# Scores over full rows, weights as column tiles, and a new split of an expert's weights in a two-block transformer kernel

## The chip, the cores and the metric

The kernel runs on one core of one Trainium2 chip. The metric is the device time of one execution in microseconds, the median of several runs; a profile comes from one further execution, recorded by the hardware profiler. The engines are PE (TensorE, with PEld for its weight loads), DVE (VectorE), ACT (ScalarE), POOL (GpSimd) and SP (SyncE), which issues nearly all DMAs.

## The reference

The input is x (1024 tokens of width 1024), a memory of 256 rows, positions, and the weights of two transformer blocks, all in fp32.

The first block adds to x, in this order: differential attention (8 heads) beside latent attention (8 heads of 64 + 32 dimensions) through one output matrix; cross attention to the memory (4 heads of 128); and a mixture of experts: 32 experts in 4 groups, each token goes to 2 experts of one group, each expert computes `(silu(h @ w_gate) * (h @ w_up)) @ w_down` with inner width 256. A norm closes the block.

The second block projects its normed input with one wide matrix and runs four branches on it:

```python
# fox: 4 heads of 64, causal, with a decay from running sums c of log-sigmoid gates
s = q @ k.T * 64**-0.5 + (c[:, None] - c[None, :]);  p = softmax(where(causal, s, -inf));  o = p @ v
# conv: a short causal convolution with gates, width 256
# mlstm: 4 heads of 64, scores weighted by exponentials of running gate sums, normed, times an output gate
# swa: 8 query heads on 2 key heads, a window of 128 keys, a bucketed position bias, a sink logit per head
```

Each branch has an output matrix; four gates of width 1024 (`tanh` halves in the kernel) weigh their sum, a merge matrix follows, and then a gated feed-forward part of width 2816.

## The kernel before

Precision. The matmuls run in fp32r, and every operand is split in two: a high part (a cast to fp32r, `hi`, on ACT) and a low part (the difference, `lo`, on DVE or POOL). A product is three matmuls, high*high, high*low and low*high (`mm3`, L111 to L113), summed in PSUM.

Weights of the projections. `load_w` (from L93) fetches one column tile of a matrix, 128 columns by `kc` blocks of 128 rows, in chunks of four blocks: one DMA on SP's queue into a `wraw` tile (3 buffers), then `hi` on ACT and `lo` on POOL. In DRAM the matrix lies row by row, so that a chunk is read as runs of 512 bytes, four for each partition.

Order. The Tile framework orders the instructions by a simulated timeline, so that projections (among them the 64 gate units of `gate_halves`, given out in small portions by `gates(n)`) are mixed on PE into the attention of the heads. SP, POOL, ACT, DVE and PE each work through their own queue in order.

Experts. `load(e)` (L1031) issues five DMAs: gate and up in two halves each, and down, into three tiles of `[128, 4, 512]` taken from a ring of twelve. `expert_in` gathers the rows of the expert's tokens with an indirect DMA, transposes and splits them, and multiplies eight weight chunks; `expert_out` applies silu, transposes, and multiplies four more chunks. Each of the twelve chunks goes through `expert_split` (L912): the high part on ACT, or on DVE for chunks 5 and 11, and the low part on POOL for chunks 0, 2, 5, 7 and 10 and on DVE for the others. Both parts lie in rings of four buffers (`whi`, `wlo`).

Scores of the second block. The queries of a head lie as a stack of 128 rows, the high part over the low part (`hq`); the keys as the high part twice (`hk`, 128 rows) and the low part once (`hkl`, 64 rows used). `stack_scores` (L1431) makes the scores of a query block against up to 512 keys with two matmuls: 128 rows (L1433), then the high query rows against the low keys, 64 rows (L1434). Fox adds the decay by a third one, minus ones against the 32 rows of its head in `ck` (L1524), and on the last chunk of a query block the causal mask, an identity of 128 rows (L1526). `attend` runs the query blocks of a head; softmax is on DVE (row maximum) and ACT (exponential), the transposed probabilities are split and multiplied with the values.

Constants. `late_consts` loads among others `iota`, `desc`, `caps` and `tok`, which only the router uses, and makes `nonesr`, the minus ones of fox.

Of the kernel before, what the change touches and what calls it, by code (L numbers as in the profile page):

```python
# [12 lines left out]
F32 = mybir.dt.float32  # L13
F32R = mybir.dt.float32r
# [8 lines left out]
P = 128  # L23
# [39 lines left out]
class K:  # L63
# [29 lines left out]
    def load_w(self, src, kc, f):  # L93

        nc = self.nc
        out = []
        for c0 in range(0, kc, 4):
            n = min(4, kc - c0)
            raw = self.t(self.wp, [P, 4, P], tag="wraw", bufs=3)[:, :n, :f]
            nc.sync.dma_start(raw, src[c0 * P:(c0 + n) * P, :].rearrange("(c p) f -> p c f", p=P))  # L100
            h = self.t(self.wp, [P, 4, P], F32R, tag="whi", bufs=4)[:, :n, :f]
            self.hi(h, raw)
            l = self.t(self.wp, [P, 4, P], F32R, tag="wlo", bufs=4)[:, :n, :f]
            self.lo(l, raw, h, nc.gpsimd)
            out += [(h[:, i], l[:, i]) for i in range(n)]
        return out
# [20 lines left out]
    def late_consts(self):  # L127
# [195 lines left out]
    def out_first(self):  # L323

        nc, tc, a = self.nc, self.tc, self.a
        with tc.tile_pool(name="mxp", bufs=1, side="right") as mp:
            for c in range(8):
                nc.sync.dma_start(self.xs[c], a["xT"][c * P:(c + 1) * P, :])
            for t0 in range(0, S, 512):
# [7 lines left out]
                for c in range(8):  # L337
                    w = self.load_w(a["w_out"][0:512, c * P:(c + 1) * P], 4, P)
# [4 lines left out]
    def out_second(self, mn, t0):  # L343
        nc, a = self.nc, self.a
        for c in range(8):
            w = self.load_w(a["w_out"][512:1024, c * P:(c + 1) * P], 4, P)
# [20 lines left out]
    def latents(self, hh, hl, sp):  # L367

        nc, a = self.nc, self.a
        for f0, f in ((0, P), (P, P), (2 * P, P), (3 * P, 64)):  # L370
            w = self.load_w(a["w_lat"][:, f0:f0 + f], 8, f)
# [7 lines left out]
    def diff_proj(self, j, hh, hl, sp):  # L379

        nc, a = self.nc, self.a
        w = self.load_w(a["w_in"][:, 1024 + j * P:1024 + (j + 1) * P], 8, P)
# [4 lines left out]
        for nmq, off in (("q", 0), ("k", 512)):  # L387
            w = self.load_w(a["w_in"][:, off + j * P:off + (j + 1) * P], 8, P)
# [106 lines left out]
    def mla_proj(self, tp):  # L495
# [58 lines left out]
        def keys(j):  # L554
            pair(self.load_w(a["w_ukv"][:, j * P:(j + 1) * P], 1, P), [ckh], [ckl], self.mkn[j])

        def queries(j):
            pair(self.load_w(a["w_uq"][:, j * P:(j + 1) * P], 2, P), cqh, cql, self.mqn[j])

        def values():  # L560
            wv = self.load_wide(a["w_ukv"][:, 512:1024])
# [20 lines left out]
        for g in range(2):  # L582
            w0 = self.load_w(a["w_uq"][:, 512 + g * P:512 + (g + 1) * P], 2, P)
            w1 = self.load_w(a["w_uq"][:, 768 + g * P:768 + (g + 1) * P], 2, P)
# [48 lines left out]
    def mem_kv(self):  # L633
# [4 lines left out]
        with tc.tile_pool(name="memp", bufs=1, side="right") as mp:  # L638
# [29 lines left out]
    def cross(self):  # L668
# [5 lines left out]
        with ExitStack() as es:  # L674
# [8 lines left out]
            with tc.tile_pool(name="chp", bufs=1, side="right") as hp:  # L683
                for t0 in range(0, S, 512):
# [3 lines left out]
                    for h in range(4):  # L688
                        w = self.load_w(a["w_mem_q"][:, h * P:(h + 1) * P], 8, P)
# [222 lines left out]
    def expert_split(self, pool, ws, n):  # L912
# [103 lines left out]
    def moe(self):  # L1016
# [4 lines left out]
        with self.wes as es:  # L1021
# [228 lines left out]
    OFF = dict(fq=0, fk=256, fv=512, cu=772, cb=1028, cc=1284, mq=1540, mk=1796, mv=2052, mo=2316, sq=2572, sk=3084, sv=3212, gates=3340)  # L1250

    def w2(self, name, j, f=P):
        o = self.OFF[name] + j * P
        return self.load_w(self.a["w_in_2"][:, o:o + f], 8, f)
# [166 lines left out]
    def head_stack(self, pool, d, h, parts, tag):  # L1421

        s = self.t(pool, [P, S], F32R, tag=tag, bufs=2)
# [7 lines left out]
    def stack_scores(self, o, q, ks, k0, kn, last=True):  # L1431
# [15 lines left out]
    def small_cols(self, hh, hl, qp, sp):  # L1447
# [4 lines left out]
        w = self.load_w(a["w_small"], 8, 12)  # L1452
# [55 lines left out]
    def fox(self, sp, j, d, ck):  # L1508
# [213 lines left out]
    def merge(self, yes, yp, sp, first):  # L1722
# [17 lines left out]
        def gated(t0, yh, yl):  # L1740
            hs = slice(t0, t0 + 512)
            mh, ml = ([self.t(mp, [P, 512], F32R, tag=f"{n}{i}") for i in range(8)] for n in ("mh", "ml"))
            for i in range(8):
# [3 lines left out]
                w = self.load_w(a["w_branch"][:, i * P:(i + 1) * P], 10, P)  # L1747
# [10 lines left out]
        def product(t0, mh, ml):  # L1758
            hs = slice(t0, t0 + 512)
            for i in range(8):  # L1760
                x = self.t(mp, [P, 512], tag="xr", bufs=2)
                nc.sync.dma_start(x, self.xd[i * P:(i + 1) * P, hs])
                w = self.load_w(a["w_merge_out_2"][:, i * P:(i + 1) * P], 8, P)
# [33 lines left out]
    def ff_in(self, sp, f0, n, act, fh, halves):  # L1797

        nc, a = self.nc, self.a
        for i in range(n):  # L1800
            cols = slice((f0 + i) * P, (f0 + i + 1) * P)
            w = self.load_w(a["w_gate_2"][:, cols], 8, P)
# [6 lines left out]
            w = self.load_w(a["w_up_2"][:, cols], 8, P)  # L1809
# [22 lines left out]
def layout(inp):  # L1832
# [7 lines left out]
    o["w_in"] = ct(f["w_in"][0])  # L1840
    lat = f["w_in"][0][:, 1536:1952]
    o["w_lat"] = ct(np.concatenate([lat, lat[:, 400:416], lat[:, 384:400]], axis=1))
    uq = f["w_mla_uq"][0].reshape(256, 8, 96)
    o["w_uq"] = ct(np.concatenate([uq[:, :, :64].reshape(256, 512), uq[:, :, 64:].reshape(256, 256),
                                   np.concatenate([uq[:, :, 80:], uq[:, :, 64:80]], axis=2).reshape(256, 256)], axis=1))
    ukv = f["w_mla_ukv"][0].reshape(P, 8, 2, 64)
    o["w_ukv"] = ct(np.concatenate([ukv[:, :, 0].reshape(P, 512), ukv[:, :, 1].reshape(P, 512)], axis=1))
    o["norm_ffn_g"] = ct(f["norm_ffn_g"].reshape(1, D))
    for name in ("w_out", "w_mem_q", "w_mem_kv", "w_mem_o"):
        o[name] = ct(f[name][0])  # L1850
# [33 lines left out]
    for name in ("w_expert_gate", "w_expert_up", "w_expert_down"):  # L1884
        o[name] = f[name][0]
# [8 lines left out]
    o["w_in_2"] = w2  # L1894
    o["w_small"] = ct(np.concatenate([w2[:, 768:772], w2[:, 2308:2312], w2[:, 2312:2316]], axis=1))
    o["b_small"] = ct(np.concatenate([f["fox_f_bias_2"][0], f["mlstm_i_bias_2"][0], f["mlstm_f_bias_2"][0]])[:, None])
    o["w_branch"] = np.concatenate([f[f"w_{n}_out_2"][0] for n in ("fox", "conv", "mlstm", "swa")], axis=0)
    for name in ("w_merge_out_2", "w_gate_2", "w_up_2", "w_down_2"):
        o[name] = f[name][0]
# [28 lines left out]
```

## Time and profile before

| what | value |
|---|---|
| median of 3 runs | 3415.92 us (3400.15 to 3417.51) |
| profiled execution: device time | 3409.51 us |
| profiled execution: span, first to last instruction | 3407.7 us |
| mean granted TensorE clock | 0.956 of 2.4 GHz |
| busy: PE, DVE, ACT, POOL | 3140.9, 1652.7, 1424.3, 1246.6 us |
| moved by DMA | 466.21 MB, mean 137 GB/s |
| packets below 2 KB, of all | 356568 of 442669 |

Busy time of PE counts a pipelined matmul from its start to its modelled end, so that neighbours overlap; the price of a matmul is the time from its start to the start of the next one. The granted clock of a stretch lies between 0.5 (1.2 GHz all the time) and 1.0 (2.4 GHz all the time). Idle time of an engine counts only where that engine sets the pace.

### The profile page before, as it was taken

What the parts mean: (1) busy time and instruction counts of PE and PEld (TensorE: products, weight loads), DVE (VectorE), ACT (ScalarE), POOL (GpSimd) and SP (SyncE); (2) the same over time, 40 slices, a digit from 0 to 9 for tenths busy, and PEclk for the clock granted to TensorE, in tenths of its full rate; (3) what the DMA queues carried; (4) which work ended last, traced back from release to release, by engine and by line L of the source; (5) the groups of instructions that cost most, each with busy time, mean ns of one, the idle gap of its engine ahead of it and who ended that gap; (6) DMA issues with size and microseconds to landing.
All of it is one profiled execution on the core that took longest, in us unless ns stands there. A gap on an engine that the chain in (4) does not pass through costs nothing.

```text
span 3407.7 us, 41840 instructions
## 1 busy us (share of the span) xinstructions
PE 3140.9 (92%) x14621; PEld 2463.5 (72%) x14621; DVE 1652.7 (48%) x3249; ACT 1424.3 (42%) x2839; POOL 1246.6 (37%) x1007
## 2 busy tenths in 40 slices
PE   6998879879968888699999999999999999999999
PEld 4786667767745555577767887778777788888887
DVE  5567985666578888653334454332356311111111
ACT  4555664544536666433333443344344322121121
POOL 3233465555446567531101111111467422222221
PEclk9998889989979999799889999999999999999999
DMA  5654645322369999344343333334565211111112
GB/s 166 212 179 144 245 119 174 91 69 83 111 224 320 329 330 303 133 122 124 96 136 108 106 105 94 92 91 160 158 204 147 85 51 43 52 44 45 51 45 79
DMA packets 442669, 466.21 MB, mean 137 GB/s; under 512 B 28344, under 2 KB 356568, under 8 KB 442456
## 3 DMA queue, kind: packets, MB, share of 16 engines
q1 hardware_dynamic: 436056, 440.44, 41.2%
q0 software_dynamic: 6400, 23.07, 2.2%
q8 instruction: 116, 1.90, 0.2%
q14 instruction: 97, 0.79, 0.1%
HBM read 349.66 MB, written 113.77 MB: 136 GB/s over the span
## 4 chain that ended last, share of the span: by engine, by line
PE 56%; DVE 1%; POOL 1%; DMA 1%; issue 0%; ACT 0%; ACTq 0%; POOLq 0%; DVEq 0%
PE mm L111 16%; PE mm L112 16%; PE mm L113 16%; PE S L1434 2%; PE T L1205 1%; PE S L1433 1%; PE T L1185 1%; PE mm L1089 1%; PE S L1524 1%; PE T L1682 0%; PE mm L164 0%; PE T L1663 0%; DMA wraw<-w_branch 0%; POOL wlo L91 0%; PE T L1104 0%
## 5 line engine op out<-in xcount | busy, mean ns | idle before, releaser
L91 POOL TENSOR_TENSOR wlo<-wraw,whi 128x512 fp32r<-128x512 f32 (+2 forms) x487 | 609.2, 1254 | 1597.6 <-ACT whi L88 1495.2
L111 PE MATMUL mm<-hh,whi 128*128 128x512 f32 (+2 forms) x1968 | 795.0, 404 | 5.5 <-DVE cql L209 2.0
L112 PE MATMUL mm<-hl,whi 128*128 128x512 f32 (+2 forms) x1968 | 793.0, 403 | 6.4 <-POOL hl L91 3.8
L113 PE MATMUL mm<-hh,wlo 128*128 128x512 f32 (+2 forms) x1968 | 790.8, 402 | 0.0
L88 ACT CAST whi<-wraw 128x512 fp32r<-128x512 f32 (+2 forms) x487 | 287.3, 594 | 737.1 <-PE mm L112 629.9
L111 PEld LDWEIGHTS mm<-hh,whi 128*128 128x128 f32 (+2 forms) x1968 | 372.9, 189 | 100.2 <-ACT hh L88 3.4
L112 PEld LDWEIGHTS mm<-hl,whi 128*128 128x128 f32 (+2 forms) x1968 | 372.6, 189 | 99.3 <-POOL hl L91 6.4
L113 PEld LDWEIGHTS mm<-hh,wlo 128*128 128x128 f32 (+2 forms) x1968 | 372.5, 189 | 89.1 <-issue 0.2
L91 POOL TENSOR_TENSOR ptl<-praw,pth 128x512 fp32r<-128x512 f32 (+2 forms) x192 | 205.7, 1075 | 233.4 <-DVE pth L1195 200.7
L91 POOL TENSOR_TENSOR wlo<-w,whi 128x512 fp32r<-128x512 f32 x160 | 225.7, 1416 | 138.8 <-ACT whi L916 106.9
L91 DVE TENSOR_TENSOR wlo<-w,whi 128x512 fp32r<-128x512 f32 x224 | 225.0, 1031 | 22.8 <-ACT whi L916 22.4
L916 ACT CAST whi<-w 128x512 fp32r<-128x512 f32 x320 | 196.2, 622 | 85.5 <-PE mm L113 51.5
L1815 DVE TENSOR_TENSOR ffgate<-ffgate,mm 128x512 f32<-128x512 f32 x44 | 30.2, 687 | 384.7 <-PE mm L113 384.7
L1185 PE MATMUL T<-ident,p 128*128 128x128 f32 x864 | 148.6, 293 | 21.2 <-DVE p L442 8.3
L1826 DVE TENSOR_TENSOR x<-mm,x 128x512 f32<-128x512 f32 x64 | 44.2, 691 | 199.1 <-PE mm L113 199.1
L1185 PEld LDWEIGHTS T<-ident,p 128*128 128x128 f32 x864 | 107.6, 150 | 45.4 <-issue 11.0
L111 PE MATMUL mm<-ah,whi 128*128 128x512 f32 x352 | 139.6, 397 | 0.3 <-DVE x L1826 0.3
L112 PE MATMUL mm<-al,whi 128*128 128x512 f32 x352 | 139.5, 396 | 0.0
L113 PE MATMUL mm<-ah,wlo 128*128 128x512 f32 x352 | 139.5, 396 | 0.0
L91 DVE TENSOR_TENSOR ptl<-T,pth 128x512 fp32r<-128x512 f32 (+2 forms) x128 | 73.1, 578 | 126.0 <-ACT pth L88 96.8
L112 PE MATMUL mm<-wlo,xh 128*112 128x512 f32 x256 | 110.7, 432 | 22.0 <-DVE wlo L91 17.6
L1194 ACT COPY praw<-T 128x512 f32<-128x512 f32 (+2 forms) x192 | 90.5, 478 | 84.2 <-PE T L1185 63.2
(485 smaller groups left out, 5858.4 us busy)
## 6 DMA issues: line engine op xcount, KB each, us to landing
wraw<-w_in SPq DMA_DIRECT2D x152, 256.0 KB, 2.9
w<-w_expert_gate SPq DMA_DIRECT2D x64, 512.0 KB, 6.4
w<-w_expert_up SPq DMA_DIRECT2D x64, 512.0 KB, 7.5
w<-w_expert_down SPq DMA_DIRECT2D x32, 1024.0 KB, 5.6
gd<-gate SPq DMA_DIRECT2D x64, 256.0 KB, 2.0
gt<-gd SPq DMA_DIRECT2D x16, 1024.0 KB, 11.6
yrow<-y SPq DMA_DIRECT2D x32, 448.0 KB, 4.2
wraw<-w_gate SPq DMA_DIRECT2D x48, 256.0 KB
```

Source lines behind the costliest of these rows:

```text
L88: self.nc.scalar.copy(out, x)
L91: (eng or self.nc.vector).tensor_tensor(out, x, h.bitcast(F32), op=OP.subtract)
L111: self.nc.tensor.matmul(out, lh, rh, start=(i == 0), stop=False)
L112: self.nc.tensor.matmul(out, lh, rl, start=False, stop=False)
L113: self.nc.tensor.matmul(out, ll, rh, start=False, stop=(i == n - 1))
L916: (nc.vector.tensor_copy if n % 6 == 5 else nc.scalar.copy)(h, w)
L1089: nc.tensor.matmul(ss[:, 2 * i:2 * i + 2], sq[:, n], sqg[:, n], start=(i == 0 and n == 0), stop=(i == 3 and n == 7))
L1185: nc.tensor.transpose(tp[:, i * P:(i + 1) * P], p[:, (k0 + i) * P:(k0 + i + 1) * P], self.c["ident"])
L1194: nc.scalar.copy(y, src)
L1205: nc.tensor.matmul(o[:, q0:256], vs[:, kb], pt[kb // 4][:, kb % 4, q0:256], start=(pt is pth and kb == 0), stop=(pt is ptl and kb == nkb - 1))
L1434: self.nc.tensor.matmul(o, q[0:64], ks[1][0:64, k0:k0 + kn], start=False, stop=last)
L1826: nc.vector.tensor_tensor(self.xs[i][:, sl], ps, self.xs[i][:, sl], op=OP.add)
```

## The change

Three things change. First, all weights that `load_w` reads are laid out before the launch as column tiles, so that each partition's part of a chunk is one run of 2 KB; the expert weights become three tensors in the layout of their SBUF tiles, read by three DMAs of 1 MB. Second, the scores of the second block: the low keys are stacked twice and multiplied with the full query stack (128 rows, which also adds the product of the two low parts), and in fox the low keys stand over the decay rows and are multiplied with the high query rows over minus ones (96 rows), which replaces two matmuls by one. For it each fox head loads the high query rows once more (`hq1`, one buffer), fills 32 rows with minus one on POOL, and copies 32 decay rows by DMA. Third, in `expert_split` all high parts go to ACT, and the low parts to DVE but for chunks 3 and 9, which go to POOL. Four constants move from `late_consts` to `moe_open`, and `nonesr` goes.

```diff
-    def load_w(self, src, kc, f):
+    def load_w(self, src, kc, f=P):
...
-            nc.sync.dma_start(raw, src[c0 * P:(c0 + n) * P, :].rearrange("(c p) f -> p c f", p=P))
+            nc.sync.dma_start(raw, src[:, c0:c0 + n])
...
-        for name, shape in (("tri", [P, P]), ("nmask", [P, P]), ("part", [P, 2]), ("iota", [P, P]), ("desc", [P, 8]), ("caps", [P, 9]), ("tok", [P, NB]), ("b_small", [12, 1])):
+        for name, shape in (("tri", [P, P]), ("nmask", [P, P]), ("part", [P, 2]), ("b_small", [12, 1])):
...
-        c["nonesr"] = self.t(pool, [P, P], F32R, tag="nonesr")
-        nc.gpsimd.tensor_scalar(c["nonesr"], c["ones"], -1.0, None, op0=OP.mult)
...
-                    w = self.load_w(a["w_out"][0:512, c * P:(c + 1) * P], 4, P)
+                    w = self.load_w(a["w_out"][c][:, 0:4], 4)
...
@@ expert_split
-        (nc.vector.tensor_copy if n % 6 == 5 else nc.scalar.copy)(h, w)
+        self.hi(h, w)
         l = self.t(pool, [P, 512], F32R, tag="wlo", bufs=4)
-        self.lo(l, w, h, nc.gpsimd if n % 5 in (0, 2) else nc.vector)
+        self.lo(l, w, h, nc.gpsimd if n in (3, 9) else nc.vector)
...
@@ moe_open
+        for name, shape in (("iota", [P, P]), ("desc", [P, 8]), ("caps", [P, 9]), ("tok", [P, NB])):
+            self.c[name] = self.t(self.moep, shape, tag=name)
+            nc.sync.dma_start(self.c[name], a[name])
...
@@ load
-                for q in range(2):
-                    for o, name in ((0, "w_expert_gate"), (256, "w_expert_up")):
-                        src = a[name][bass.ds(e, 1)][:, q * 512:(q + 1) * 512]
-                        nc.sync.dma_start(ws[q][:, :, o:o + 256], src.rearrange("o (c p) f -> p (o c) f", p=P))
-                nc.sync.dma_start(ws[2].rearrange("p (c n) f -> p c (n f)", c=2), a["w_expert_down"][bass.ds(e, 1)].rearrange("o (c p) f -> p (o c) f", p=P))
+                for i, w in enumerate(ws):
+                    nc.sync.dma_start(w.rearrange("p c f -> p (c f)"), a["w_expert"][i][bass.ds(e, 1)].rearrange("o p f -> p (o f)"))
...
-    def head_stack(self, pool, d, h, parts, tag):
+    def head_stack(self, pool, d, h, parts, tag, bufs=2):
...
-        return self.head_stack(pool, kd, h, (0, 0), "hk"), self.head_stack(pool, kd, h, (1,), "hkl")
+        return self.head_stack(pool, kd, h, (0, 0), "hk"), self.head_stack(pool, kd, h, (1, 1), "hkl")
...
-        self.nc.tensor.matmul(o, q, ks[0][:, k0:k0 + kn], start=True, stop=False)
-        self.nc.tensor.matmul(o, q[0:64], ks[1][0:64, k0:k0 + kn], start=False, stop=last)
+        for i, k in enumerate(ks):
+            self.nc.tensor.matmul(o, q, k[:, k0:k0 + kn], start=(i == 0), stop=(i == 1))
...
@@ fox
-            qs, ks = self.head_stack(sp, qd, h, (0, 1), "hq"), self.head_keys(sp, kd, h)
+            qs, kh = self.head_stack(sp, qd, h, (0, 1), "hq"), self.head_stack(sp, kd, h, (0, 0), "hk")
+            q1, kl = self.head_stack(sp, qd, h, (0,), "hq1", 1), self.head_stack(sp, kd, h, (1,), "hkl")
+            nc.gpsimd.memset(q1[64:96, :].bitcast(F32), -1.0)
+            nc.sync.dma_start(kl[64:96, :].bitcast(F32), ck[32 * n:32 * n + 32, :].bitcast(F32))
...
-                self.stack_scores(o, qs[:, qb * P:(qb + 1) * P], ks, k0, kn, last=False)
-                nc.tensor.matmul(o, c["nonesr"][r], ck[r, k0:k0 + kn], start=False, stop=not last)
+                q = slice(qb * P, (qb + 1) * P)
+                nc.tensor.matmul(o, qs[:, q], kh[:, k0:k0 + kn], start=True, stop=False)
+                nc.tensor.matmul(o, q1[0:96, q], kl[0:96, k0:k0 + kn], start=False, stop=not last)
...
@@ layout
+    def tiles(w, f=P):
+        return ct(w.reshape(w.shape[0] // P, P, w.shape[1] // f, f).transpose(2, 1, 0, 3))
...
+    gu = np.concatenate([f["w_expert_gate"][0], f["w_expert_up"][0]], axis=2).reshape(32, 2, 4, P, 512).transpose(1, 0, 3, 2, 4).reshape(2, 32, P, 2048)
+    down = f["w_expert_down"][0].reshape(32, 2, P, D).transpose(0, 2, 1, 3).reshape(1, 32, P, 2048)
+    o["w_expert"] = np.concatenate([gu, down], axis=0)
```

## Rows read from the trace of the kernel before

**Rows 1.** Busy time by stretch: length, engines, PEclk, DMA share, GB/s.

```profile
980.00:1400.00 420.00, 342.94 (x1529) 231.82 (x1529) 346.59 (x486) 275.08 (x480) 256.01 (x191) 0.97 0.84 279
...
1579.00:1720.00 141.00, 140.24 (x621) 103.30 (x619) 48.18 (x101) 52.87 (x119) 16.65 (x13) 0.90 0.34 97
1720.00:1786.00 66.00, 66.00 (x263) 44.72 (x263) 24.02 (x42) 21.76 (x48) 5.15 (x4) 0.87 0.44 127
1786.00:2087.00 301.00, 300.59 (x1539) 240.87 (x1538) 147.53 (x486) 124.96 (x273) 43.78 (x34) 1.00 0.36 105
...
2708.00:3408.00 700.00, 695.51 (x2968) 558.48 (x2966) 104.13 (x145) 124.51 (x212) 159.13 (x132) 1.00 0.18 52
```

**Rows 2.** PE's timeline in fox's first pair: start us, us, instruction.

```profile
1597.10 0.45 PE L1433 MATMUL S<-hk,hq 128*128 128x512 f32 x1
1597.48 0.50 PE L1434 MATMUL S<-hkl,hq 64*128 64x512 f32 x1
1597.91 0.49 PE L1524 MATMUL S<-gb,nonesr 32*128 32x512 f32 x1
1598.34 0.38 PE L1433 MATMUL S<-hk,hq 128*128 128x256 f32 x1
...
1599.27 0.33 PE L1526 MATMUL S<-nmaskr,identr 128*128 128x128 f32 x1
1599.43 0.45 PE L111 MATMUL mm<-hh,whi 128*128 128x512 f32 x1
1599.72 0.39 PE L112 MATMUL mm<-hl,whi 128*128 128x512 f32 x1
```

**Rows 3.** PE's timeline in the first block's latent attention.

```profile
704.20 0.40 PE L623 MATMUL S<-sk,sq 96*128 96x512 f32 x1
704.44 0.23 PE L625 MATMUL S<-nmaskr,identr 128*128 128x128 f32 x1
```

**Rows 4.** Line L1524: duration ns min/median/max, first and last start, forms.

```profile
L1524 PE MATMUL S<-gb,nonesr x48: 321/490/789, 1580.0 to 1779.2; 32*128 32x512 f32 x24, 32*128 32x128 f32 x8, 32*128 32x256 f32 x8, 32*128 32x384 f32 x8
```

**Rows 5.** PE's timeline in fox's second pair.

```profile
1761.90 0.50 PE L1434 MATMUL S<-hkl,hq 64*128 64x512 f32 x1
1762.34 0.50 PE L1524 MATMUL S<-gb,nonesr 32*128 32x512 f32 x1
```

**Rows 6.** PE's timeline in the sliding-window branch.

```profile
2145.94 0.28 PE L1433 MATMUL S<-hk,hq 128*128 128x256 f32 x1
2146.15 0.38 PE L1434 MATMUL S<-hkl,hq 64*128 64x256 f32 x1
2146.46 0.50 PE L111 MATMUL mm<-hh,whi 128*128 128x512 f32 x1
2146.80 0.40 PE L112 MATMUL mm<-hl,whi 128*128 128x512 f32 x1
```

**Rows 7.** DVE in the timeline of the experts, the same place of two experts.

```profile
1200.12 4.15 DVE L91 TENSOR_TENSOR wlo<-w,whi 128x512 fp32r<-128x512 f32 x4
...
1212.53 4.14 DVE L91 TENSOR_TENSOR wlo<-w,whi 128x512 fp32r<-128x512 f32 x4
```

**Rows 8.** Busy time in 50 us of the experts; columns as in rows 1.

```profile
1150.00:1200.00 50.00, 41.34 (x185) 27.71 (x186) 40.74 (x54) 34.80 (x61) 30.29 (x25) 1.00 1.00 330
```

**Rows 9.** Tiles wlo and whi, 1050 to 1350 us: duration ns min/median/max.

```profile
L91 DVE TENSOR_TENSOR wlo<-w,whi x172: 676/694/1787, 1050.0 to 1349.5; 128x512 fp32r<-128x512 f32 x172
L91 POOL TENSOR_TENSOR wlo<-w,whi x122: 1275/1329/1965, 1050.5 to 1348.9; 128x512 fp32r<-128x512 f32 x122
...
L916 ACT CAST whi<-w x244: 617/621/645, 1050.0 to 1348.8; 128x512 fp32r<-128x512 f32 x122
...
L916 DVE CAST whi<-w x49: 412/434/3086, 1049.7 to 1347.1; 128x512 fp32r<-128x512 f32 x49
```

**Rows 10.** DMA rate in 40 slices of 930 to 1000 us.

```profile
GB/s 100 0 274 135 180 157 152 0 180 238 342 411 402 384 384 400 424 387 379 405 383 431 391 386 426 419 129 0 236 63 0 0 0 0 0 122 257 150 0 187
```

**Rows 11.** The chain that ended last, in the merge: start us, us, what.

```profile
2460.01 5.43 DMA wraw<-w_branch
```

More of the change, by code (lines that the diff above doesn't have):

```diff
@@ L370, in latents @@
         for f0, f in ((0, P), (P, P), (2 * P, P), (3 * P, 64)):
-            w = self.load_w(a["w_lat"][:, f0:f0 + f], 8, f)
+            w = self.load_w(a["w_rot"][0] if f < P else a["w_lat"][f0 // P], 8, f)
             def sink(ps, t0, n):
@@ L386, in diff_proj @@
         out = []
-        for nmq, off in (("q", 0), ("k", 512)):
-            w = self.load_w(a["w_in"][:, off + j * P:off + (j + 1) * P], 8, P)
+        for nmq, off in (("q", 0), ("k", 4)):
+            w = self.load_w(a["w_in"][off + j], 8)
             d = self.dp.tile([P, 4, S], F32, name=self.nm("ds"))
@@ L554, in keys @@
         def keys(j):
-            pair(self.load_w(a["w_ukv"][:, j * P:(j + 1) * P], 1, P), [ckh], [ckl], self.mkn[j])
+            pair(self.load_w(a["w_uk"][j], 1), [ckh], [ckl], self.mkn[j])
         def queries(j):
-            pair(self.load_w(a["w_uq"][:, j * P:(j + 1) * P], 2, P), cqh, cql, self.mqn[j])
+            pair(self.load_w(a["w_uq"][j], 2), cqh, cql, self.mqn[j])
         def values():
-            wv = self.load_wide(a["w_ukv"][:, 512:1024])
+            wv = self.load_wide(a["w_uv"])
             for tt in range(NB):
@@ L582, in mla_proj @@
         for g in range(2):
[L583 to L584 removed]
+            w0 = self.load_w(a["w_uq"][4 + g], 2)
+            w1 = self.load_w(a["w_uq"][6 + g], 2)
             y = self.t(tp, [P, S], tag="qpy")
@@ L1247, in row_sums, with w2 @@
         return self.t(pool, [P, NB, 2], tag="rowsum", bufs=2)
[L1250 to L1254, printed above, removed]
+    OFF = dict(fq=0, fk=2, fv=4, cu=6, cb=8, cc=10, mq=12, mk=14, mv=16, mo=18, sq=20, sk=24, sv=25, gates=26)
+    def w2(self, name, j):
+        return self.load_w(self.a["w_in_2"][self.OFF[name] + j], 8)
     def second_mix(self):
@@ L1419, in qk_steps @@
         yield d
-    def head_stack(self, pool, d, h, parts, tag):
-        s = self.t(pool, [P, S], F32R, tag=tag, bufs=2)
+    def head_stack(self, pool, d, h, parts, tag, bufs=2):
+        s = self.t(pool, [P, S], F32R, tag=tag, bufs=bufs)
         for i, p in enumerate(parts):
@@ L1428, in head_keys, with stack_scores @@
     def head_keys(self, pool, kd, h):
[L1429 to L1434 removed]
+        return self.head_stack(pool, kd, h, (0, 0), "hk"), self.head_stack(pool, kd, h, (1, 1), "hkl")
+    def stack_scores(self, o, q, ks, k0, kn):
+        for i, k in enumerate(ks):
+            self.nc.tensor.matmul(o, q, k[:, k0:k0 + kn], start=(i == 0), stop=(i == 1))
     def row_bcast(self, dst, cols):
@@ L1746, in gated @@
                 nc.scalar.activation(g, g, AF.Tanh, scale=0.5)
-                w = self.load_w(a["w_branch"][:, i * P:(i + 1) * P], 10, P)
+                w = self.load_w(a["w_branch"][i], 10)
                 for b, part in enumerate(branches):
@@ L1839, in layout @@
     o["positions"] = ct(f["positions"])
-    o["w_in"] = ct(f["w_in"][0])
+    o["w_in"] = tiles(f["w_in"][0][:, :1536])
     lat = f["w_in"][0][:, 1536:1952]
-    o["w_lat"] = ct(np.concatenate([lat, lat[:, 400:416], lat[:, 384:400]], axis=1))
+    o["w_lat"] = tiles(lat[:, :384])
+    o["w_rot"] = tiles(np.concatenate([lat[:, 384:], lat[:, 400:416], lat[:, 384:400]], axis=1), 64)
     uq = f["w_mla_uq"][0].reshape(256, 8, 96)
-    o["w_uq"] = ct(np.concatenate([uq[:, :, :64].reshape(256, 512), uq[:, :, 64:].reshape(256, 256),
-                                   np.concatenate([uq[:, :, 80:], uq[:, :, 64:80]], axis=2).reshape(256, 256)], axis=1))
+    o["w_uq"] = tiles(np.concatenate([uq[:, :, :64].reshape(256, 512), uq[:, :, 64:].reshape(256, 256),
+                                      np.concatenate([uq[:, :, 80:], uq[:, :, 64:80]], axis=2).reshape(256, 256)], axis=1))
     ukv = f["w_mla_ukv"][0].reshape(P, 8, 2, 64)
-    o["w_ukv"] = ct(np.concatenate([ukv[:, :, 0].reshape(P, 512), ukv[:, :, 1].reshape(P, 512)], axis=1))
+    o["w_uk"] = tiles(ukv[:, :, 0].reshape(P, 512))
+    o["w_uv"] = ct(ukv[:, :, 1].reshape(P, 512))
     o["norm_ffn_g"] = ct(f["norm_ffn_g"].reshape(1, D))
-    for name in ("w_out", "w_mem_q", "w_mem_kv", "w_mem_o"):
-        o[name] = ct(f[name][0])
+    for name in ("w_out", "w_mem_q", "w_mem_o"):
+        o[name] = tiles(f[name][0])
+    o["w_mem_k"] = tiles(f["w_mem_kv"][0][:, :512])
+    o["w_mem_v"] = ct(f["w_mem_kv"][0][:, 512:])
     inv = np.array(INV_FREQ, np.float32)
@@ L1893, in layout @@
     w2 = f["w_in_2"][0]
-    o["w_in_2"] = w2
-    o["w_small"] = ct(np.concatenate([w2[:, 768:772], w2[:, 2308:2312], w2[:, 2312:2316]], axis=1))
+    o["w_in_2"] = tiles(np.concatenate([w2[:, :768], w2[:, 772:2308], w2[:, 2316:]], axis=1))
+    o["w_small"] = tiles(np.concatenate([w2[:, 768:772], w2[:, 2308:2312], w2[:, 2312:2316]], axis=1), 12)
     o["b_small"] = ct(np.concatenate([f["fox_f_bias_2"][0], f["mlstm_i_bias_2"][0], f["mlstm_f_bias_2"][0]])[:, None])
-    o["w_branch"] = np.concatenate([f[f"w_{n}_out_2"][0] for n in ("fox", "conv", "mlstm", "swa")], axis=0)
+    o["w_branch"] = tiles(np.concatenate([f[f"w_{n}_out_2"][0] for n in ("fox", "conv", "mlstm", "swa")], axis=0))
     for name in ("w_merge_out_2", "w_gate_2", "w_up_2", "w_down_2"):
-        o[name] = f[name][0]
+        o[name] = tiles(f[name][0])
     o["nmask"] = np.where(i[None, :] <= i[:, None], 0.0, -BIG).astype(np.float32)
```

26 lines of the change are left out of this document (11 added, 15 removed).

## The prediction

> **What bounds the kernel now.** I read the stages first (busy time and granted clock by stretch), because the diff touches three places that lie in different ones. From 1579 us to 2087 us, the second block's fox and mLSTM branches, TensorE is busy without a hole: 140.24 of 141 us, 66 of 66, 300.59 of 301, while DVE, ACT and POOL are at half or less and the DMA engines at 34 to 44% [rows 1]; the sliding window behind them looks the same. What shortens the PE stream there shortens the kernel, as long as the other engines keep up. From 980 to 1400 us, the experts, no engine is full: PE 343 of 420 us, DVE 347, ACT 275, POOL 256 [rows 1]. Something else sets that pace, and the second reading looks for it. The feed-forward part at the end is pure PE: 2968 matmuls in 700 us, 0.236 us from one 512-column matmul to the next at clock 1.00 [rows 1]. I use 0.235 as the price of 512 full-row columns, 0.117 for 256, 0.06 for 128.
>
> The next view is PE's timeline in the first fox branch, start to start (busy times overlap and hide this) [rows 2]. A chunk of 512 keys costs 0.38 us for L1433 (128 rows), 0.43 for L1434 (64 rows) and 0.43 for L1524 (32 rows): 1.24 us where three full-row matmuls would take 0.71. The reader is to see that the price grows hardly at all with width: the three 256-column ones take 0.93 (1598.34 to 1599.27), so 0.31 each against 0.117. The diagonal mask L1526 pays 0.16 instead of 0.06, and the projection matmul behind it 0.29 instead of 0.235. So each change of the number of rows costs 0.15 to 0.2 us.
>
> **Scores, part by part.** The diff replaces 64+32 rows in fox by one matmul of 96 rows (query high part over the low keys, with minus one over the decay rows), and in mLSTM and sliding-window attention the 64-row matmul by one of 128 rows whose keys are stacked twice. Does 96 count as full? In the first block's latent attention L623 has 96 rows and hands over to the 128-row L625 in 0.24 us, the plain cadence, nothing lost [rows 3]. So I price 96 rows as full.
>
> Fox has 48 chunks: 24 of 512, 8 each of 384, 256 and 128 columns [rows 4]. Before 1.24 us at 512 and 0.93 at 256, so by the same line 1.09 at 384 and 0.78 at 128. After: two passes, 0.47, 0.35, 0.235, 0.12. Saved: 24 x 0.77 + 8 x (0.74 + 0.70 + 0.66) = 35.3 us, and 32 diagonals with the matmul behind them, 0.16 each, 5.1: **40.4 us**.
>
> One rule speaks against this part. Matmuls of 64 rows and 32 rows that lie on separate row groups of the array could overlap, and the change would give that up. In fox's second pair the decay rows are 64 to 127 and the low keys 0 to 63, quite separate, yet L1434 and L1524 start 0.44 us apart [rows 5], as in the first pair where they share rows. The Trainium skill, page "TensorE: Matmul & The Clock Gate", Part 3, says that such matmuls run concurrently. By that rule the pair would have cost one step of 0.43 us instead of two in half the heads, 12 x 0.43 + 4 x (0.37 + 0.31 + 0.25), and this part would bring 9 us less; the trace shows no overlap, so I go by the rows.
>
> mLSTM has fox's 48 chunks again, and the sliding window one chunk for each of 8 heads and 8 query blocks: 112. At 256 columns L1433 takes 0.21, L1434 0.31 and the projection behind it 0.34, together 0.86 us [rows 6]; at full rows 0.117 + 0.117 + 0.235 = 0.47. Saved 0.39 x 112 = **43.7 us**. Chunks of 512 follow the same pattern with the same fixed loss; I bound the term by 0.3 and 0.46 each: 34 to 52.
>
> The clock: fox's two stretches have a granted clock of 0.90 and 0.87 where mLSTM after them has 1.00 [rows 1], although that also is full of attention. Lost there: 141 x 0.10 + 66 x 0.13 = 22.7 us. The dips to 1.2 GHz fall where the score triples stand close together, PE nominally busy but mostly waiting for the row change. With the triples gone I take 18 of 22.7 back; bounds 0 and 22.7.
>
> What the change adds: per fox head one more 64-row query load, a copy of 32 decay rows, and a memset of minus one on POOL; per key set in the other branches one more 64-row half. Together 4 x 256 + 4 x 128 + 6 x 256 KB, 3 MB, in stretches with the DMA engines at a third [rows 1]; hidden, and if not, about 10 us at 300 GB/s. The new query tile has one buffer: its load, and the SP queue behind it (gate weights, gate stores), waits until the previous head's last score. PE has gate projections between heads, so I charge 1 us at each of 3 boundaries, **3 us** lost (bounds 0 and 18, a whole landing of up to 6 us each).
>
> **Experts.** One expert takes 12.4 us: the same four DVE subtractions come at 1200.12 and 1212.53 [rows 7]. A busy table of 50 us there shows PE 41.34, DVE 40.74, ACT 34.80, POOL 30.29 [rows 8]. The column to read is DVE's low-part subtraction: median 694 ns but longest 1787, and the four of rows 7 take 4.15 us, not 2.8; the same form on POOL takes 1.33 [rows 9]. DVE's long ones are those under a POOL instruction: they wait for it. So the SBUF work of the two adds instead of overlapping: 7 x 0.694 + 2 casts x 0.434 + 5 x 1.329 = 12.4 us, the period. That is the bound. The new division: 12 casts on ACT, 10 subtractions on DVE, 2 on POOL. DVE plus POOL: 10 x 0.694 + 2 x 1.329 = 9.6. ACT: 34.80/50 x 12.4 = 8.6, plus 2 x 0.62 [rows 9] = 9.9, the next bound; ACT waits 3.8 us per expert today (12.4 less 8.6), for buffers that PE holds, which come free sooner with DVE, and for PE's results, which don't; I leave a third of it, 1.3: 11.2 us. Weights and rows are 4.1 MB per expert; the loads ran at 380 to 430 GB/s at the start of the stage [rows 10], 10.1 us, so DMA stays behind ACT. Saved 1.2 x 32 = **38 us**; bounds 0 (ACT's casts in line with its waits keep 12.4) and 2.3 x 32 = 74 (DMA).
>
> **Column tiles.** Every weight load keeps its bytes but has one 2 KB run per partition instead of four of 512 B. In PE-bound stages the weights land well before use. It matters where PE's chain ends in a load: in the merge, 5.43 us for w_branch behind 1 MB of gates [rows 11]. I take **3 us**, bounds 0 and 10. The Trainium skill, page "DMA: Bandwidth & Descriptors", Specifications, gives 512 B as the least size for line rate; by that the new layout would bring 0 here, and no run here shows which. The constants that move to a later pool, and the dropped constant, cost nothing: they are loaded long before use, under full PE.
>
> **Sum**, against the profiled execution's 3409.5 us: 40.4 + 43.7 + 18 - 3 + 38 + 3 = 140, so 3269.5. The runs' median is 6.4 above that execution; I add 6: **3275 us**.
>
> **Rivals.** (1) The experts don't gain: ACT, in order, holds the casts behind its silu, copies and PSUM reads; its idle time is buffers held by PE as much as DVE. For it: ACT would be 80% busy at 12.4; against: DVE plus POOL explains the period to the tenth. 3275 + 38 = 3313. (2) The 96-row matmul still breaks the stream, and the clock dips stay: fox then saves only L1524's own time, 24 x 0.43 + 8 x (0.37 + 0.31 + 0.25) = 18 us instead of 58. For it: no row shows 96 rows straight behind 128 in one score; against: L623. 3315. (3) The expert stage is better than thought and runs at the DMA's pace, 10.1 us: 3240. (4) Slower: the experts become a chain of ACT cast, DVE subtraction and three matmuls with little overlap. One chunk is 0.62 + 0.69 + 0.70 = 2.0 us, 24 us for the 12 of an expert; the four buffers allow 6. With the second block's 102 us won, the kernel is slower from 12.4 + 102/32 = 15.6 us per expert on, that is when fewer than 1.54 chunks are in flight; at 1.4 it is 17.1 us and 3409.5 + 6 - 102 + 4.7 x 32 = 3464. For it: ACT now stands in all 12 chunks, and waits for PE in order; against: PE's own 41 of 50 us already needs more than two in flight. (5) The separate row groups did overlap in fox's second pair, hidden in how matmul ends are modelled: 3275 + 9 = 3284. That is the overlap of the Trainium skill named above.
>
> **How the numbers follow.** Forecast 0.60 (3250 to 3300); (1) 0.17; (2) 0.10; (3) 0.06; (4) 0.03; (5) 0.01; the rest, 0.03, no measurable change, should several gains fail at once. Some 0.5%, 17 us, is what a measurement tells here. Faster 0.94, within 0.5% 0.03, slower 0.03. Range 3235 to 3325: from (3) to beyond (1) and (2).
>
> **What would show it.** Right: L1524 gone, scores 0.23 to 0.25 us apart at 512 columns, clock near 1.00 in both fox stretches, PE still full there; an expert in 11 to 11.5 us, DVE's mean subtraction near 0.8. Wrong: PE holes at the start of a fox head (the single buffer), dips of the clock that stay, a period of 12.4 with ACT at 80%, or DMA waits in front of ACT's casts.

## The result, and the profile after

The changed kernel takes 3258.33 us (median of 4 runs, 3254.11 to 3260.77) beside 3415.62 for the kernel before on the same chip: ratio 0.9548, 95% interval 0.9518 to 0.9578. That is faster by 157 us; the forecast was 3275, with a range of 3235 to 3325. The profiled execution took 3256.75 us, its span is 3255.0, the mean granted clock 0.963.

Stages are compared by the first and last start of a line that both kernels have: silu in the experts, the causal mask in fox, the exponential in the sliding window.

| stretch | before, us | after, us | difference | forecast |
|---|---|---|---|---|
| start to the first transpose of the experts | 995.0 | 989.1 | -5.9 | 0 |
| experts, first to last silu (31 steps) | 381.1 | 330.3 | -50.8 | -38 |
| fox, first to last mask | 199.7 | 153.5 | -46.2 | -55 |
| last mask to last exponential (mLSTM, sliding window) | 544.6 | 497.1 | -47.5 | -44 |
| everything else | 1287.3 | 1285.0 | -2.3 | -3 |

Busy time by stretch after, the answer to [rows 1]: the experts, fox, mLSTM, the sliding window.

```profile
980.00:1345.00 365.00, 323.14 (x1512) 231.92 (x1512) 300.67 (x508) 299.58 (x544) 128.45 (x99) 0.98 0.87 321
1522.00:1676.00 154.00, 148.92 (x812) 124.83 (x812) 66.05 (x135) 71.65 (x163) 24.60 (x20) 0.98 0.47 140
1676.00:1940.00 264.00, 261.45 (x1423) 221.91 (x1423) 145.85 (x479) 118.68 (x260) 41.38 (x32) 1.00 0.39 122
1940.00:2173.00 233.00, 233.00 (x1249) 198.92 (x1248) 89.68 (x242) 100.79 (x252) 42.24 (x32) 1.00 0.33 104
```

Fox's clock rose from 0.90 and 0.87 to 0.98. But PE, which had no hole there before, now idles 5.1 of 154 us. Both show in PE's timeline of the first fox head and the border to the second, which answers to [rows 2]:

```profile
1540.71 0.48 PE L1525 MATMUL S<-hk,hq 128*128 128x512 f32 x1
1541.03 0.39 PE L1526 MATMUL S<-hkl,hq 96*128 96x512 f32 x1
1541.26 0.40 PE L1525 MATMUL S<-hk,hq 128*128 128x512 f32 x1
1541.49 0.40 PE L1526 MATMUL S<-hkl,hq 96*128 96x512 f32 x1
1541.73 0.22 PE L1528 MATMUL S<-nmaskr,identr 128*128 128x128 f32 x1
1542.39 0.30 PE L1184 MATMUL T<-ident,p 128*128 128x128 f32 x1 [0.44 <-DVE ptl L91]
1543.81 0.33 PE L1525 MATMUL S<-hk,hq 128*128 128x128 f32 x1 [1.12 <-ACT p L1538]
1545.19 0.45 PE L1526 MATMUL S<-hkl,hq 96*128 96x128 f32 x1 [1.05 <-DMA hq<-qkd]
...
1549.17 0.63 PE L112 MATMUL mm<-hl,whi 128*128 128x512 f32 x1
1549.60 0.63 PE L113 MATMUL mm<-hh,wlo 128*128 128x512 f32 x1
```

Read the starts. A chunk of 512 keys costs 0.23 us for the 128 rows and 0.23 for the 96 rows, 0.47 in all where it was 1.24, and the mask follows at the same cadence. Then come three short waits; after them projection matmuls start 0.43 us apart, which is the lower clock, 1.2 GHz.

The sliding window, the answer to [rows 6], shows two score matmuls and the projection behind them:

```profile
1987.41 0.28 PE L1432 MATMUL S<-hk,hq 128*128 128x256 f32 x1
1987.52 0.28 PE L1432 MATMUL S<-hkl,hq 128*128 128x256 f32 x1
1987.64 0.39 PE L113 MATMUL mm<-hh,wlo 128*128 128x512 f32 x1
1987.87 0.39 PE L111 MATMUL mm<-hh,whi 128*128 128x512 f32 x1
```

0.11 + 0.12 + 0.23 = 0.46 us, where it was 0.86 and 0.47 was forecast.

The experts, the answers to [rows 8, 9], in three views: 50 us of busy time; the low parts, duration ns min/median/max; the silu's first and last start.

```profile
1150.00:1200.00 50.00, 46.25 (x212) 32.67 (x212) 40.04 (x64) 43.68 (x78) 16.14 (x15) 1.00 1.02 381
```

```profile
L91 DVE TENSOR_TENSOR wlo<-w,whi x233: 675/692/1782, 1049.4 to 1299.6; 128x512 fp32r<-128x512 f32 x117
L91 POOL TENSOR_TENSOR wlo<-w,whi x47: 1262/1303/1879, 1049.5 to 1297.8; 128x512 fp32r<-128x512 f32 x47
```

```profile
L943 ACT ACTIVATE hid<-mm x32: 374/377/385, 1001.2 to 1331.5; 112x256 f32<-112x256 f32 x32
```

(1331.5 - 1001.2) / 31 = 10.65 us an expert, where the same view of before gives 12.29. The longest DVE subtraction still takes 1782 ns, but the mean over the line fell from 1033 to 769 ns. PE is now busy for 92% of those 50 us.

### The profile page after: what moved, and what is told of

It reads as the page before. It is cut to its first block, busy times and chain, and to the rows that moved or that the text cites. A ratio compares the mean times of both kernels' runs of the same rounds, so it can differ in the third digit from the quotient of the medians.

```text
span 3255.0 us, 41632 instructions
## 1 busy us (share of the span) xinstructions
PE 3015.5 (93%) x14573; PEld 2435.8 (75%) x14573; DVE 1612.2 (50%) x3281; ACT 1447.6 (44%) x2903; POOL 1119.0 (34%) x914
## 4 chain that ended last, share of the span: by engine, by line
PE 54%; DMA 2%; DVE 1%; ACT 1%; POOL 1%; issue 1%; SPq 0%; ACTq 0%; DVEq 0%; POOLq 0%
PE mm L111 16%; PE mm L112 16%; PE mm L113 16%; PE T L1204 1%; PE T L1184 1%; PE S L1432 1%; PE mm L1088 1%; DMA gt<-gd 1%; PE T L1684 0%; POOL wlo L91 0%; PE mm L162 0%; PE T L1665 0%; PE T L1103 0%; DVE gt L1755 0%; PE S L1526 0%
## 5 line engine op out<-in xcount | busy, mean ns | idle before, releaser
L111 PE MATMUL mm<-hh,whi 128*128 128x512 f32 (+2 forms) x1968 | 786.4, 400 | 8.3 <-DVE cql L207 2.0
L112 PE MATMUL mm<-hl,whi 128*128 128x512 f32 (+2 forms) x1968 | 785.1, 399 | 6.6 <-POOL hl L91 4.1
L88 ACT CAST whi<-w 128x512 fp32r<-128x512 f32 x384 | 232.8, 624 | 49.2 <-PE mm L113 19.5
L91 DVE TENSOR_TENSOR wlo<-w,whi 128x512 fp32r<-128x512 f32 x320 | 238.5, 774 | 29.5 <-ACT whi L88 26.4
L91 POOL TENSOR_TENSOR wlo<-w,whi 128x512 fp32r<-128x512 f32 x64 | 90.3, 1412 | 199.2 <-ACT whi L88 135.7
L1184 PEld LDWEIGHTS T<-ident,p 128*128 128x128 f32 x864 | 105.7, 147 | 47.5 <-ACT praw L1193 10.9
L435 ACT ACTIVATE p<-p,st 128x128 f32<-128x128 f32 (+7 forms) x128 | 99.3, 777 | 35.2 <-DVE st L434 34.0
```

The costliest lines, as they stand in the source:

```text
L88: self.nc.scalar.copy(out, x)
L91: (eng or self.nc.vector).tensor_tensor(out, x, h.bitcast(F32), op=OP.subtract)
L111: self.nc.tensor.matmul(out, lh, rh, start=(i == 0), stop=False)
L112: self.nc.tensor.matmul(out, lh, rl, start=False, stop=False)
L435: nc.scalar.activation(p[:, :nk], p[:, :nk], AF.Exp, scale=-1.0, bias=st[:, m:m + 1], accum_out=(den[:, qb, h:h + 1], st[:, 2:3])[m])
L1184: nc.tensor.transpose(tp[:, i * P:(i + 1) * P], p[:, (k0 + i) * P:(k0 + i + 1) * P], self.c["ident"])
```

## The experiments

Eleven kernels ran, in three groups, each on one chip beside runs of the kernel before: the first four (3406.77 us), the next four (3409.09) and the last three (3408.25). The change itself was not timed beside the first eight; beside the last three, on the chip of the first four, it took 3255.84, so a difference to its 3258.33 in the first two groups holds to some 3 us.

**The new split alone**, in the kernel before:

```diff
-        (nc.vector.tensor_copy if n % 6 == 5 else nc.scalar.copy)(h, w)
+        self.hi(h, w)
...
-        self.lo(l, w, h, nc.gpsimd if n % 5 in (0, 2) else nc.vector)
+        self.lo(l, w, h, nc.gpsimd if n in (3, 9) else nc.vector)
```

> The kernel before with the new division of an expert's weights alone (old layout, old scores). Theory: DVE and POOL exclude each other on SBUF, and this alone sets the pace; the period per expert falls from 12.3 us to about 10.7 and the time by 45 to 52 us. Rival: the DMA share of 1.00 in the stage means that the loads set the pace and the new layout brought the gain; then under 20 us. A second rival: half and half, 25 to 35 us.

Measured: 3362.46 us, ratio 0.9871 (0.9846 to 0.9897), 44 us less. The silu line and fox's busy row:

```profile
L945 ACT ACTIVATE hid<-mm x32: 374/378/387, 997.4 to 1327.2; 112x256 f32<-112x256 f32 x32
```

```profile
1522.00:1731.00 209.00, 208.24 (x861) 148.99 (x860) 70.73 (x140) 73.40 (x165) 21.82 (x17) 0.86 0.33 98
```

The experts take 10.64 us each with the old loads as with the new ones, so the whole gain of that stage is the split's and none the layout's. The stage gave 51 us and the kernel 44. The old fox, whose code this kernel doesn't touch, took 209.1 us from first to last mask at clock 0.86, where it took 199.7 at 0.90 in the profile of before. That would make up for the 7 us, but no profile of the kernel before was taken beside this run, so it isn't shown. What the two profiles do show is that the old fox has no fixed length, and that the longer one had the lower clock.

**The change with the old split** (the diff above, reversed).

> The changed kernel with the old division put back. Theory: the period returns to 12.3 to 12.4 us and the time rises by 45 to 52 us over the changed kernel, to about 3308. Rival (the layout of the loads brought it): it rises by under 20 us, to at most 3278.

Measured: 3304.96 us, ratio 0.9701 (0.9679 to 0.9723), 47 more than the change; the experts are back at 12.33 us each (silu from 1003.6 to 1385.8). So the split is worth 44 us of the kernel's time without the other two edits and some 47 with them.

**The score rows alone**: `head_stack`, `head_keys`, `stack_scores` and `fox` of the change, and its constants, in the kernel before.

> The kernel before with the scores over full rows alone (and the constants moved to make room). Theory: 94 us less than before, since fox, mLSTM and the sliding window are full of PE work and no load or split plays a part: about 3322. Rival: lighter weight loads take part in it (the gate weights that fill PE between the scores); then 75 to 85 us less.

Measured: 3299.65 us, ratio 0.9694 (0.9668 to 0.972), 107 less, more than either theory. Its stages give 95: fox 153.5 us (-46.2 against the profile of before), the two other branches 495.4 (-49.2). The 12 us that are left are not settled, since no profile of the kernel before was taken beside this run. Against the run with the new split alone, which has the old scores and ran on the same chip, the same stages give 108: 55.6 in fox and 52.0 in the two other branches (547.4 there). So old scores that ran slower there than in the profile of before can account for it.

**Fox's 96 rows as 64 and 32 again**, in the change. Both lie on their own rows:

```diff
-                nc.tensor.matmul(o, q1[0:96, q], kl[0:96, k0:k0 + kn], start=False, stop=not last)
+                nc.tensor.matmul(o, q1[0:64, q], kl[0:64, k0:k0 + kn], start=False, stop=False)
+                nc.tensor.matmul(o, q1[64:96, q], kl[64:96, k0:k0 + kn], start=False, stop=not last)
```

> The changed kernel, but fox's 96-row matmul issued as two of the same operands: 64 rows (rows 0 to 63) and 32 rows (rows 64 to 95). Theory: every change of the number of rows costs 0.15 to 0.2 us, so a 512-column chunk is back at 1.24 us; 35 to 50 us more than the changed kernel with the clock's dips, about 3300. Rival (separate row groups overlap): the 32-row matmul runs beside the 64-row one; 0 to 5 us more.

Measured: 3309.98 us, ratio 0.9717 (0.9696 to 0.9739), 52 more than the change. PE's timeline and fox's busy row:

```profile
1572.39 0.48 PE L1525 MATMUL S<-hk,hq 128*128 128x512 f32 x1
1572.80 0.50 PE L1526 MATMUL S<-hkl,hq 64*128 64x512 f32 x1
1573.23 0.49 PE L1527 MATMUL S<-hkl,hq 32*128 32x512 f32 x1
1573.66 0.33 PE L1529 MATMUL S<-nmaskr,identr 128*128 128x128 f32 x1
1573.82 0.45 PE L1204 MATMUL T<-pth,hvs 128*128 128x256 f32 x2
```

```profile
1524.00:1731.00 207.00, 203.91 (x858) 146.41 (x857) 70.67 (x140) 72.67 (x164) 23.40 (x20) 0.87 0.34 106
```

0.41, 0.43, 0.43 and 0.16 for the mask are the steps of before to 0.03 us, and the clock dips are back too (0.87). Fox's masks span 206.6 us, 53 more. The two row groups, 0 to 63 and 64 to 95, start 0.43 us apart, and the mask follows the second after 0.43 more, as in the kernel before: they don't overlap. The rule of the Trainium skill, "TensorE: Matmul & The Clock Gate", Part 3, that matmuls on separate row groups run concurrently doesn't show here. Both add into one PSUM region in this kernel, and they differ in their number of rows; no run tried separate regions or equal numbers, so why they don't overlap stays open.

**Column tiles alone**, with the three expert loads: the change with old scores and old split.

> The kernel before with the column tiles and the three-transfer expert loads alone; scores and the split of an expert's weights as before. Theory of the prediction: the loads were nowhere late, so the tiles are worth the 3 us of its sum, 3402 to 3406 beside 3407 (at most 10: 3397). Rival one: the score rows alone gave 107 us and the split alone 44, 151 together, and the whole change gave 157, so the tiles give the 6 that are left, about 3401. Rival two: the tiles cost time before the experts. There the two kernels with the old layout began the experts' transposes at 985.0 and 981.6 us, the three with the new one at 988.2 to 989.1, so the time is about 5 us more, 3412; the stages behind the experts then show no difference in either direction.

Measured: 3412.79 us, ratio 1.0013 (0.9996 to 1.0031): no gain. The silu and the mask:

```profile
L944 ACT ACTIVATE hid<-mm x32: 378/386/389, 1004.7 to 1385.3; 112x256 f32<-112x256 f32 x32
```

```profile
L1522 PE MATMUL S<-nmaskr,identr x32: 326/327/475, 1577.1 to 1776.8; 128*128 128x128 f32 x32
```

380.6 and 199.7 us, as before. The layout does what it says: 212011 packets in place of 442669, and a weight chunk of `w_in` lands in 2.6 us in place of 2.9 (medians). A 1 MB load of gates in the merge, whose own layout is as before, lands in 7.1 in place of 11.6. The time of the kernel shows nothing of it. The Trainium skill, "DMA: Bandwidth & Descriptors", Specifications, by which the 512-byte runs already had line rate, foretold no gain, and the time agrees; that the landings did get shorter is not in it. The rival that the tiles cost time before the experts isn't settled. Its 3412 us is close to what was measured, but the interval runs from 1.4 us less to 10.6 more than before. On the chip of the first and last group the first transpose came at 981.6 and 985.0 us in two kernels with the old layout and at 983.7 to 989.0 in five with the new one; in the profile of before it came at 995.0. So the 5.9 us of the table's first line aren't shown to be the change's, and a cost of a few us can't be ruled out.

**How the split works: none, two or four low parts on POOL, and casts back on DVE.** Three kernels from the change:

```diff
-        self.lo(l, w, h, nc.gpsimd if n in (3, 9) else nc.vector)
+        self.lo(l, w, h, nc.vector)
...
+        self.lo(l, w, h, nc.gpsimd if n in (0, 3, 6, 9) else nc.vector)
...
-        self.hi(h, w)
+        (nc.vector.tensor_copy if n % 6 == 5 else nc.scalar.copy)(h, w)
```

> The changed kernel with all 12 low parts of an expert on VectorE, none on GpSimd. By the prediction's model the port that the two engines share asks for 12 x 0.694 = 8.3 us an expert in place of 9.6. Theory: the experts now go at 10.65 us each, above the 9.6 that the port asks for, so it isn't the bound any more, and VectorE's own work of 8.3 + 2 us (its two low parts of the activations and the product) still lies under 10.65: within 4 us of 3258. Rival one, the port still sets the pace with a fixed loss behind it (10.65 - 9.6 = 1.05): 9.4 us an expert, 40 us less, about 3218. Rival two, VectorE becomes the bound, since 12 low parts stand in its own order with waits between them: 11.2 an expert, 17 us more, about 3275.

> The changed kernel with four of an expert's 12 low parts on GpSimd (numbers 0, 3, 6 and 9) in place of two. The port then asks for 8 x 0.694 + 4 x 1.33 = 10.9 us an expert in place of 9.6. Theory, the port is a floor under the pace and nothing more: 10.9 lies just above today's 10.65, so the time is 3258 + 31 x 0.25, about 3266. Rival one, the port with a fixed loss of 1.05 behind it: 11.9 us an expert, 40 us more, about 3298. Rival two, the casts on ScalarE and the matmuls set the pace, and GpSimd's parts only lie beside them: no change, 3258.

> The changed kernel with casts 5 and 11 of an expert back on VectorE as before; the low parts stay divided as in the change. This parts the change of the split into its two halves. The port asks for 9.6 + 2 x 0.434 = 10.5 us an expert, ScalarE's work falls from 9.2 to 8.0 us (two casts of 0.62). Theory, the port is a floor and the fewer parts on GpSimd are what gave the 51 us: 10.5 lies under 10.65, so no change, 3254 to 3262. Rival one, ScalarE's casts are the bound now: 1.2 us an expert less, down to the matmuls' 9.85 us, about 3230. Rival two, taking the casts off VectorE was what gave the gain: the 12.3 us of before come back in good part, over 3285.

Measured: none 3241.79 (ratio 0.953, 0.9503 to 0.9557), four 3272.51 (0.9609, 0.9584 to 0.9634), casts on DVE 3264.72 (0.9594, 0.9569 to 0.962). The period of an expert from the silu line, beside what DVE and POOL ask for together when they exclude each other (0.694 us for a low part on DVE, 1.33 on POOL, 0.434 for a cast on DVE):

| kernel | DVE and POOL ask, us | period, us | PE busy in 1150 to 1200 us |
|---|---|---|---|
| before | 12.4 | 12.29 | 41.34 |
| four on POOL | 10.9 | 11.21 | 46.06 |
| casts on DVE | 10.5 | 11.05 | 43.96 |
| the change | 9.6 | 10.65 | 46.25 |
| none on POOL | 8.3 | 10.23 | 48.41 |

With none on POOL, the same three views:

```profile
1150.00:1200.00 50.00, 48.41 (x225) 34.44 (x223) 45.10 (x80) 44.55 (x84) 4.42 (x4) 1.00 1.02 390
```

```profile
L91 DVE TENSOR_TENSOR wlo<-w,whi x290: 680/689/695, 1050.0 to 1299.6; 128x512 fp32r<-128x512 f32 x145
```

```profile
L943 ACT ACTIVATE hid<-mm x32: 375/377/399, 1000.0 to 1317.2; 112x256 f32<-112x256 f32 x32
```

The long subtractions are gone: 695 ns at most, where four on POOL show

```profile
L91 DVE TENSOR_TENSOR wlo<-w,whi x179: 674/693/3254, 1049.0 to 1299.0; 128x512 fp32r<-128x512 f32 x179
L91 POOL TENSOR_TENSOR wlo<-w,whi x90: 1263/1307/1861, 1049.2 to 1298.3; 128x512 fp32r<-128x512 f32 x90
```

So what stretched them was POOL's work, as the prediction read from [rows 9]. In the trace of before, from 1050 to 1300 us, each of the 64 DVE subtractions above 750 ns lies under a subtraction on POOL; the 37 that lie under none are all shorter. Neither theory of a floor nor that of a fixed loss holds. Each us less that the two engines ask for gives 0.3 to 0.7 us, less and less towards PE's floor: 48.41/50 x 10.23 = 9.9 us. With casts on DVE, ACT is relieved and the period still grows, so ACT isn't the bound; with none on POOL its work stays (44.55/50 x 10.23 = 9.1 us, 9.3 in the change) and the period falls. The run with casts on DVE also splits the 51 us: 12 came from taking the two casts off DVE (342.4 against 330.3 us), 39 from POOL's parts going from five to two.

**Toward a better kernel.** The change once more; the change with `hq1` kept for all four heads, its rows of minus one written once and its load issued behind the head's other loads; and both that and no low part on POOL. The second edit:

```diff
-            q1, kl = self.head_stack(sp, qd, h, (0,), "hq1", 1), self.head_stack(sp, kd, h, (1,), "hkl")
-            nc.gpsimd.memset(q1[64:96, :].bitcast(F32), -1.0)
+            kl = self.head_stack(sp, kd, h, (1,), "hkl")
...
             vs = self.head_values(sp, vd, h)
+            if n == 0:
+                self.q1 = self.t(sp, [P, S], F32R, tag="hq1", bufs=1)
+                nc.gpsimd.memset(self.q1[64:96, :].bitcast(F32), -1.0)
+            q1 = self.q1
+            nc.sync.dma_start(q1[0:64, :].bitcast(F32), qd[0, 64 * h:64 * h + 64, :])
```

> The changed kernel as it is, once more, beside the next two on the same chip: 3253 to 3261, as in its first timing (3258).

> The changed kernel with one edit in the forgetting attention: the tile hq1 is kept for all four heads, its rows of -1 are written once, and its load is issued behind all other loads of a head. Theory: between the heads of a pair the changed kernel lost time since the load of hq1, and behind it in SP's order the key loads, had to wait for the last score matmul of the head before, then for a fill of 0.94 us. In the first pair TensorE did little from 1542.4 to 1545.2 us (1.12 us put down to ScalarE's weights, 1.05 to the load) and ran at the lower clock until 1550.5, which cost about 3.4 us. With the load alone behind that matmul the hole and the dip go: 3 to 7 us less, 3251 to 3255. Rival: the hole begins with the wait of 1.12 us for ScalarE, which stays, and the load still lands some 2 us behind the last matmul: 0 to 1 us less, with the dip as it was.

> Both edits: no low part of an expert's weights on GpSimd, and hq1 loaded last with its rows of -1 written once. If the two gains stand in different stages they add: 13 us of the first and 3 to 7 of the second, 3238 to 3242. If the second is nothing: 3245. If the first was only a chip's difference (it was not timed beside the changed kernel): 3251 to 3258.

Measured: the change 3255.84 (ratio 0.9551, 0.9536 to 0.9567), hq1 last 3255.41 (0.955, 0.9531 to 0.9568), both edits 3241.20 (0.9509, 0.9493 to 0.9524). The load last changes nothing that the time shows; PE's timeline at the same border:

```profile
1540.77 0.22 PE L1532 MATMUL S<-nmaskr,identr 128*128 128x128 f32 x1
1541.44 0.30 PE L1184 MATMUL T<-ident,p 128*128 128x128 f32 x1 [0.45 <-DVE ptl L91]
1542.86 0.33 PE L1529 MATMUL S<-hk,hq 128*128 128x128 f32 x1 [1.11 <-ACT p L1542]
1544.36 0.33 PE L1530 MATMUL S<-hkl,hq 96*128 96x128 f32 x1 [1.18 <-DMA hq<-qkd]
```

The three waits stand there as before, and the dip behind them, about half as long: the clock of the 10 us behind the mask is 0.83, 0.66 in the change. Fox took 152.2 us, 153.6 in the change; but the kernel with four low parts on POOL, which loads `hq1` as the change does, took 152.2 too, so that isn't shown to be the edit's. The load was still issued just behind the start of the last score matmul of the head before (1540.96 against 1540.77 us), so the rival was right. A second buffer for hq1 wasn't tried. What is left is no low part on POOL: with both edits the kernel takes 14.6 us less than the change on the same chip, and is faster than the one before and than the change.

## Why the prediction was right, and where its terms were off

The time and its sign were right: 3258 in a range of 3235 to 3325, and 17 us below the point. The mechanisms were those forecast, but two sizes were off: the experts gave 13 us more than their term, fox 9 less. These errors partly cancel, and 6 us that nothing forecast came before the experts, so part of the closeness is luck.

**Score rows.** Right, in price and place: 0.47 us a chunk in fox and 0.46 in the sliding window with its projection. The 96 rows count as full, as L623 in [rows 3] promised, so rival 2 fell. Rival 5, that separate rows had overlapped, fell with the run of 64 and 32 rows.

**Clock.** Fox had 40.4 for rows and 18 for the clock, less 3 for the borders of heads: 55. Measured 46.2. The term for the borders was too small, if all new idle time of PE is put down to it: that went from 0.8 to 5.1 us, 2.6 of it in the three waits at the first border. That leaves 50.5 us for rows and clock together, where 58.4 were forecast. No run parts the two, but the traces do, roughly. In the kernel before, a chunk at the lower clock reads:

```profile
1660.42 0.63 PE L1433 MATMUL S<-hk,hq 128*128 128x512 f32 x1
1660.98 0.79 PE L1434 MATMUL S<-hkl,hq 64*128 64x512 f32 x1
1661.70 0.79 PE L1524 MATMUL S<-gb,nonesr 32*128 32x512 f32 x1
1662.42 0.80 PE L1433 MATMUL S<-hk,hq 128*128 128x512 f32 x1
```

A step of 64 or 32 rows takes 0.72 us there, 0.43 in [rows 2]: 1.7 times as long, not twice. So the 22.7 us, which took half of the time at the lower clock as lost, were too much. Between the first and the last mask the clock was low for some 40 us before and 7 after. Against the median of the same step at full clock, those stretches cost about 17 us before and 4 after; this is an estimate from all start-to-start times of the two traces. By it the clock gave back 13 us, where 18 were forecast, and 37 are left for the rows, where 40.4 were forecast: both terms were too large, the clock's more.

The clock's term also has no single value. In three profiles the old fox took 199.7, 199.7 and 209.1 us, and the 64 and 32 rows 206.6, while nine profiles with the new rows lie between 152.2 and 153.9. So the edit also removed most of the spread. A change of row counts alone doesn't make the dips: mLSTM before alternated 128 and 64 rows at clock 1.00 [rows 1].

**mLSTM and sliding window.** 47.5 against 43.7, inside the bounds of 34 to 52.

**Experts.** The step that was mis-sized: "ACT: ... 9.9, the next bound" and the third of its waits on top, 11.2 us an expert. ACT's work measured 43.68/50 x 10.65 = 9.3, and it isn't the bound. (Its waits came out as forecast, 1.35 us an expert, but by luck: they didn't set the pace.) The next bound is PE at 9.9, approached gradually while DVE and POOL's sum of 9.6 still costs a part. The pace is 10.65, the gain 50.8 in place of 38. The first half of the reasoning, that DVE and POOL add up and set the 12.3 us, is what three kernels now show. Rival 1 (no gain), rival 3 (the pace of the loads) and rival 4 (a chain of cast, subtraction and matmuls) fell: PE is busy for 92% of the 50 us shown and for 97% with none on POOL, and in neither trace did a cast wait for a load, at 390 GB/s too.

**Column tiles.** 3 us forecast, none measured: the interval leaves a gain of 1.4 us at most, so the lower bound was right.

## What to carry to other kernels

Look at start-to-start times where matmuls of different row counts alternate: pad or stack them to one count, even when that multiplies more, and the clock that dipped among them may come back too. Before giving work to POOL to relieve DVE, compare the shortest and the longest duration of the same form on DVE; where the long ones fall under POOL's instructions, the two add, and the work is cheaper on the faster engine alone. When that sum is cut, look for the next bound among all engines, PE too: the time saved shrinks gradually as the next one is approached.

## What was not expected of the hardware

A DVE subtraction took up to 3254 ns with four low parts on POOL, where the same form alone took 689: it can wait for two POOL instructions, 1307 ns each. That one started at 1049.01 us and ended at 1052.26, 0.56 behind the second of two POOL subtractions in a row (1049.17 to 1050.47, 1050.41 to 1051.70). The Trainium skill, "SBUF — State Buffer", Who interferes with whom, says that two-input operations of VectorE from SBUF contend with GpSimd's reads and that the second one blocks fully; the durations agree.

The DMA engines' busy share reads 1.00 in the experts before, at 330 GB/s [rows 8], and 1.02 at 390 GB/s with none on POOL, where a load of 1 MB took 12.5 us to land. So a share of 1.00 didn't mean that the loads were the bound: with none on POOL the same stage moved more, and no cast waited for a load.
